# Output, attention output, up and down projections by seven half-size products, with the mixing on GpSimd

## The chip, the cores and the metric

One core of a Trainium2 chip runs the kernel in one launch. The metric is the device time of that launch in microseconds. TensorE (PE) does the matmuls into PSUM, its weight loads (PEld) run beside them; VectorE (DVE), ScalarE (ACT) and GpSimd (POOL) work elementwise; SyncE (SP) issues most DMAs.

## The reference

A decoder block for 512 tokens and a width of 1024, all in float32:

```python
h = rmsnorm(x, norm_mix_g);  proj = h @ w_in           # 1024 -> 5120 + 3 * 1024
branches = stack([conv_out, sb_out, ret_out])           # three mixers of width 512
merged = sum(sigmoid(gates) * (branches @ w_branch))
x = x + merged @ w_o                                    # 1024 x 1024
h = rmsnorm(x, norm_xa_g)
x = x + memory_attention(h, mem_n, w_xq, w_xkv, w_out)  # w_out: 1024 x 1024
h = rmsnorm(x, norm_mlp_g)
x = x + square(relu(h @ w_up)) @ w_down                 # 1024 -> 4096 -> 1024
return rmsnorm(x, final_g)
```

## The kernel before, in words

**Precision.** Every large product is made of three matmuls in a fast float32 format: each operand is split into a high part (a cast on ScalarE) and a low part (a subtraction on VectorE), and high x high, high x low and low x high are added in PSUM. `split` (L221) does this for activations, `parts_of` (L103) for weights: ScalarE writes the high part at L111, VectorE subtracts at L112. `mm3` (L232) issues the three matmuls.

**Weights.** They come as blocks of 128x1024 (512 KB) from SyncE's queue into `w_raw` (three buffers). `Stream` lists all blocks in the order of their use; `run_plan` (L203) goes through the plan of work items, and ahead of each item prepares the weights up to two steps beyond what the item needs (`AHEAD`). A block of kind `Plain` is one step, one `parts_of`. A block of kind `Seven` is two loads and four steps; two of them mix weights first: `combo` (L134) forms two differences of 512 columns on VectorE into `w_mix`.

**Two ways to multiply.** `proj_t` (weights stationary, 128x512 or 128x256 matmuls) and `proj_m` (tokens stationary, 512 weight columns moving) take all products as they are. `seven` (L282) makes two blocks of 128 output columns from seven half-size products instead of eight (rows of the weight, columns and tokens are halved; sums and differences of the halves are multiplied, and the results added). It takes its mixed activations from `Mixes`, made once per normed input on VectorE, and uses 128x256 matmuls (L290). Half of the gate columns and 24 of the 32 up columns go that way.

**The stages that the change touches**, in order:
- gates: `gated` (L722) sums the three gated branches into `mg` and splits the sum into `mgs`.
- output projection: `proj_norm` (L842) runs `items_m` (L322) over `w_o` twice, once for each half of the 1024 output columns: four row blocks of tokens, eight blocks of 128 weight rows, three matmuls of 128x512 each. All eight accumulate in PSUM, and then VectorE adds the bank into `x` (L836): eight adds for each 1024 rows of weight and 512 columns. Then the norm and the transposes follow for each block of tokens.
- cross attention: `xa_out` (L937) makes the heads' outputs and splits them; `proj_norm` runs again, over `w_xo`.
- MLP: the up columns come in rounds of eight (`first_up`, `up7`), each followed by `items_m` over 1024 rows of `w_down`. The up results go through relu, a square and a split into `u`.
- end: the last pass over `w_down` goes by token blocks, so that `final` (L1028) norms and stores one block while TensorE does the next.

The order of instructions on each engine is settled when the program is built, by a scheduler that starts from the order of the plan. An engine goes through its list in order.

## Time and profile before

| | us |
|---|---|
| median of three runs (1033.85 to 1033.92) | 1033.91 |
| the profiled execution, its own time | 1033.71 |
| its span, first to last instruction | 1032.0 |
| output projection, from its first to its last matmul | 472 to 520 |
| cross-attention output projection | 637 to 682 |
| matmuls of the down projection | 729 to 1025 |

A row of a table of windows gives a stretch of the span, its length, and then for each engine the busy time in it with the number of instructions. A row of a timeline gives start, duration, engine, line, operation, what is written and read, and in brackets the idle time before it and what ended it. Names are those of tiles in the program: `w_raw` and `w_mix` are weights before the split, `w_part` after it, `mm` and `p` are PSUM banks, `sb_`, `r_` and `cv_` belong to the three mixers. "128x512" is partitions by elements.

### The profile page before, as it was taken

The numbers are of one execution on the slowest core, as the hardware profiler recorded it, in microseconds if no ns is written. First come the engines' busy times: TensorE is split into PE (matmuls) and PEld (weight loads), VectorE is DVE, ScalarE is ACT, GpSimd is POOL, SyncE is SP. The second block draws the span as 40 slices with busy tenths as digits, with TensorE's granted clock in tenths as the row PEclk, the third lists the DMA queues.
The fourth block names the chain that finished last, engine by engine and source line by source line (L and its number), as shares of the span: only waits on it lengthen the run. The fifth ranks groups of instructions, "written<-read, shape, count | busy, mean of one in ns | idle before, by whom it ended". The sixth has DMA issues, their size and how long they took to land.

```text
span 1032.0 us, 14325 instructions
## 1 busy us (share of the span) xinstructions
PE 1015.5 (98%) x5636; PEld 884.9 (86%) x5636; DVE 648.8 (63%) x992; ACT 500.7 (49%) x887; POOL 66.2 (6%) x118
## 2 busy tenths in 40 slices
PE   6999999999999999999999999999999999999997
PEld 4888888888888889998898888898889989989985
DVE  5567777856563796784584555466947566565643
ACT  6465567766532154463463444345416624643741
POOL 1101112321110000000100000000000000000000
PEclk9999999999999999999999999999999999999999
DMA  6322233213122212335354213223222321332222
GB/s 265 103 102 81 83 104 102 82 42 123 62 87 79 100 62 83 103 119 198 133 184 163 82 47 118 81 83 123 86 79 82 125 92 71 124 123 80 103 85 81
DMA packets 29876, 106.33 MB, mean 103 GB/s; under 512 B 3569, under 2 KB 3569, under 8 KB 29809
## 3 DMA queue, kind: packets, MB, share of 16 engines
q1 hardware_dynamic: 27216, 98.05, 27.7%
q10 hardware_dynamic: 2592, 7.37, 2.0%
q8 instruction: 44, 0.72, 0.3%
q14 instruction: 24, 0.19, 0.1%
HBM read 103.31 MB, written 2.10 MB: 102 GB/s over the span
## 4 chain that ended last, share of the span: by engine, by line
PE 97%; DMA 1%; DVE 0%; ACT 0%; SPq 0%; issue 0%; DVEq 0%; POOLq 0%; POOL 0%
PE mm L235 24%; PE mm L234 24%; PE mm L236 24%; PE p L290 17%; PE at L385 1%; PE o L546 1%; PE aT L512 1%; DMA w_raw<-in_w_in_dram 1%; PE z L488 1%; PE z L489 0%; PE xsc L236 0%; PE xsc L235 0%; PE xsc L234 0%; PE ro L693 0%; PE sc L667 0%; PE xpp L929 0%
## 5 line engine op out<-in xcount | busy, mean ns | idle before, releaser
L112 DVE TENSOR_TENSOR w_part<-w_raw,w_part 128x1024 fp32r<-128x1024 f32 (+1 forms) x180 | 210.9, 1176 | 168.1 <-PE mm L235 75.2
L111 ACT CAST w_part<-w_raw 128x1024 fp32r<-128x1024 f32 (+1 forms) x180 | 180.6, 1006 | 135.2 <-PE mm L236 79.1
L234 PE MATMUL mm<-hT_h,w_part 128*128 128x512 f32 (+1 forms) x512 | 193.6, 379 | 0.0
L235 PE MATMUL mm<-hT_l,w_part 128*128 128x512 f32 (+1 forms) x512 | 193.3, 378 | 0.0
L236 PE MATMUL mm<-hT_h,w_part 128*128 128x512 f32 (+1 forms) x512 | 193.0, 378 | 0.0
L290 PE MATMUL p<-mix_h,w_part 128*128 128x256 f32 x576 | 112.2, 283 | 0.5 <-ACT sv_s L297 0.5
L236 PEld LDWEIGHTS mm<-hT_h,w_part 128*128 128x128 f32 x512 | 96.4, 188 | 17.1
L234 PEld LDWEIGHTS mm<-hT_h,w_part 128*128 128x128 f32 x512 | 96.2, 188 | 16.8
L235 PEld LDWEIGHTS mm<-hT_l,w_part 128*128 128x128 f32 x512 | 96.5, 188 | 16.4
L235 PE MATMUL mm<-w_part,u_h 128*128 128x512 f32 x256 | 99.8, 390 | 0.0
L234 PE MATMUL mm<-w_part,u_h 128*128 128x512 f32 x256 | 98.6, 390 | 0.0
L236 PE MATMUL mm<-w_part,u_l 128*128 128x512 f32 x256 | 98.2, 389 | 0.0
L290 PEld LDWEIGHTS p<-mix_h,w_part 128*128 128x128 f32 x576 | 93.4, 192 | 1.4 <-ACT sv_s L297 0.7
L290 PE MATMUL p<-hT_h,w_part 128*128 128x256 f32 x432 | 84.4, 283 | 0.0
L290 PE MATMUL p<-mix_l,w_part 128*128 128x256 f32 x288 | 81.5, 283 | 0.0
L290 PEld LDWEIGHTS p<-hT_h,w_part 128*128 128x128 f32 x432 | 70.1, 192 | 0.8
L111 ACT CAST w_part<-w_mix 128x1024 fp32r<-128x1024 f32 x36 | 37.8, 1051 | 55.9 <-PE mm L235 37.5
L112 DVE TENSOR_TENSOR w_part<-w_mix,w_part 128x1024 fp32r<-128x1024 f32 x36 | 44.0, 1221 | 26.7 <-ACT w_part L111 20.0
L290 PE MATMUL p<-hT_l,w_part 128*128 128x256 f32 x216 | 60.7, 283 | 0.0
L236 PEld LDWEIGHTS mm<-w_part,u_l 128*128 128x128 f32 x256 | 48.1, 188 | 9.8
L235 PEld LDWEIGHTS mm<-w_part,u_h 128*128 128x128 f32 x256 | 48.1, 188 | 9.5
L234 PEld LDWEIGHTS mm<-w_part,u_h 128*128 128x128 f32 x256 | 47.9, 188 | 9.5
(211 smaller groups left out, 1813.2 us busy)
## 6 DMA issues: line engine op xcount, KB each, us to landing
w_raw<-in_w_in_dram SPq DMA_DIRECT2D x52, 512.0 KB, 3.4
w_raw<-in_w_up_dram SPq DMA_DIRECT2D x32, 512.0 KB, 3.6
w_raw<-in_w_down_dram SPq DMA_DIRECT2D x32, 512.0 KB, 3.4
w_raw<-in_w_br_dram SPq DMA_DIRECT2D x12, 512.0 KB, 3.4
w_raw<-in_w_gate_dram SPq DMA_DIRECT2D x12, 512.0 KB, 3.5
w_raw<-in_w_o_dram SPq DMA_DIRECT2D x8, 512.0 KB, 3.5
w_raw<-in_w_xk_dram SPq DMA_DIRECT2D x8, 512.0 KB, 4.2
w_raw<-in_w_xv_dram SPq DMA_DIRECT2D x8, 512.0 KB, 3.5
```

The lines of the kernel that those rows point to most:

```text
L111: act.copy(out=wh, in_=src)
L112: dve.tensor_tensor(out=wl, in0=src, in1=wh.bitcast(F32), op=ALU.subtract)
L234: te.matmul(ps, lh, rh, start=first, stop=False)
L235: te.matmul(ps, lh, rl, start=False, stop=False)
L236: te.matmul(ps, ll, rh, start=False, stop=last)
L290: te.matmul(ps[:, :256], x[:, k, :], y, start=first and k == 0 and i == 0, stop=k == 3 and i == 2, skip_group_check=True)
L385: te.transpose(ps[:, k * P:(k + 1) * P], xn[:, c * P:(c + 1) * P], ident)
L488: te.matmul(z[:, :s], q[:, e, tsl], S["skh", hp][:, e, :s], start=True, stop=False)
L512: te.transpose(aps[:, sb * P:(sb + 1) * P], a[:, sb * P:(sb + 1) * P], ident)
L546: te.matmul(dst, vv, rhs, start=sb == 0 and i == 0, stop=sb == nblk and i == 1, skip_group_check=True)
```

## The change

The weights `w_o`, `w_xo` and `w_down` are now taken in rounds of 512 rows, and each round by seven half-size products (rows of the weight by 256, output columns by 512, tokens by 256). Tokens are stationary and 512 weight columns move, so the matmuls stay 128x512: 7 x 12 of them a round in place of 96.
- `Wide` prepares a round's weights: four loads, seven steps, each with a `parts_of` of 1024 columns; four additions or subtractions of 128x1024 mix them first, on GpSimd, partly in place in `w_raw`.
- `Pairs` holds the activations of a round for the products; `make` mixes two blocks of 128 rows with one GpSimd instruction of 512 elements and two of 256, and splits the results (three times 512, once 256).
- `items_w` issues the products P1 to P7, each for two blocks of 128 tokens. P1, P6, P7 and P4 accumulate one after another in one PSUM bank for each token block, P5 and P3 in another, P2 has its own. After each product VectorE adds the bank, as it stands, into one quarter of `x`: 14 adds of 128x512 a round.
- `Seven` has its four weight combinations on GpSimd, too; its first product's signs are turned so that ScalarE has one copy less.
- The up columns go in pairs, and a round of `w_down` follows every second pair; the square of relu is taken on ScalarE. The four plain up columns that ran with 512 tokens at once run in two halves of 256, since hT now lies in blocks of 256 tokens (`Blocks`).
- The end norms two token blocks together. `w_raw` has four buffers for three, `w_part` ten for eleven. The weights are packed to suit.

```diff
@@ -31,7 +31,7 @@
...
-RAWS, WBUFS, AHEAD = 3, 11, 2
+RAWS, WBUFS, AHEAD = 4, 10, 2
...
+    def minus(out, a, b):
+        pool.tensor_tensor(out=out, in0=a, in1=b, op=ALU.subtract)
+    def plus(out, a, b):
+        pool.tensor_tensor(out=out, in0=a, in1=b, op=ALU.add)
+    def mix_raw():
+        return wpool.tile([P, CW], F32, name="w_mix", bufs=2)
...
-        def combo(self, a0, a1, b0, b1):
-            x = wpool.tile([P, CW], F32, name="w_mix", bufs=2)
-            dve.tensor_tensor(out=x[:, :512], in0=a0, in1=a1, op=ALU.subtract)
-            dve.tensor_tensor(out=x[:, 512:], in0=b0, in1=x[:, :512] if b1 is None else b1, op=ALU.subtract)
-            return x
...
         def s1(self, raw):
-            ra, rb = raw
-            self.x1 = self.combo(ra[:, 512:], ra[:, :512], rb[:, :512], ra[:, 512:])
-            return parts_of(self.x1)
+            l, r = raw[0][:, :512], raw[0][:, 512:]
+            b22, b21 = raw[1][:, :512], raw[1][:, 512:]
+            self.x = mix_raw()
+            minus(l, r, l)
+            plus(r, r, b22)
+            plus(self.x[:, :512], b22, l)
+            minus(self.x[:, 512:], b21, self.x[:, :512])
+            return parts_of(raw[0])
         def s2(self, raw):
-            rb = raw[1]
-            return parts_of(self.combo(rb[:, :512], self.x1[:, :512], rb[:, 512:], None))
+            return parts_of(self.x)
...
+    ORDER = ("P1", "P5", "P6", "P3", "P2", "P7", "P4")
...
+    class Wide:
...
+        def __init__(self, t, c):
+            self.loads = [(t, c + i) for i in range(4)]
+            self.need = (1, 2, 3, 3, 4, 4, 4)
+            self.steps = [lambda raw, n=n: self.step(raw, n) for n in range(7)]
+            self.parts = []
+        def step(self, raw, n):
+            src = raw[(0, 0, 0, 2, 3, 1, 0)[n]]
+            if n == 1:
+                minus(raw[0], raw[1], raw[0])
+            elif n == 2:
+                src = self.x = mix_raw()
+                plus(src, raw[2], raw[0])
+                plus(raw[1], raw[1], raw[2])
+            elif n == 6:
+                src = self.x
+                minus(src, raw[3], src)
+            return parts_of(src)
...
-                    self.steps.append((e, st, first + (len(e.loads) if i else 1)))
+                    self.steps.append((e, st, first + e.need[i]))
...
+    class Pairs:
+        def __init__(self):
+            self.b = unit("pr_b", (P, 2, 2, 256))
+            self.w = [{}, {}]
+        def make(self, e, s, u):
+            def put(names, src):
+                w = unit("pr", (P, 2, 2, 256))
+                split(w[:, 0], w[:, 1], src)
+                for i, n in enumerate(names):
+                    self.w[e][n] = w[:, 0, i, :], w[:, 1, i, :]
+            v = scr("pr_v", (P, 2, 256))
+            pool.tensor_tensor(out=v, in0=u[:, 0:1, :].broadcast_to([P, 2, 256]), in1=s, op=ALU.subtract)
+            put(("A11", "A22"), s)
+            minus(u[:, 0, :], s[:, 0, :], v[:, 1, :])
+            put(("S3", "S1"), v)
+            hi, lo = self.w[e]["A12"] = self.b[:, e, 0, :], self.b[:, e, 1, :]
+            split(hi, lo, u[:, 1, :])
+            minus(u[:, 1, :], u[:, 1, :], u[:, 0, :])
+            put(("S2", "S4"), u)
...
+    LEFT = dict(P1="A11", P2="A12", P3="S4", P4="A22", P5="S1", P6="S2", P7="S3")
+    TO = dict(P1=(0, 0), P2=(0, 0), P3=(0, 1), P4=(2, 0), P5=(2, 1), P6=(0, 1), P7=(2, 1))
...
+    def items_w(src, c, pairs, after=lambda p: None):
...
+        acc = {}
+        for n, p in enumerate(ORDER):
+            def fn(w, p=p):
+                wh, wl = wv(w, 2)
+                blocks = pairs().w
+                for i in range(2):
+                    if p == "P2":
+                        ps = mmps("p2")
+                    else:
+                        bank = "p3" if p in ("P5", "P3") else "p1"
+                        if p in ("P1", "P5"):
+                            acc[bank, i] = atps(bank)
+                        ps = acc[bank, i]
+                    tok = slice(i * P, (i + 1) * P)
+                    for k in range(2):
+                        ah, al = [x[:, tok] for x in blocks[k][LEFT[p]]]
+                        for m, (x, y) in enumerate(((ah, wh), (ah, wl), (al, wh))):
+                            te.matmul(ps, x, y[:, k, :], start=p in ("P1", "P5", "P2") and k == 0 and m == 0,
+                                      stop=k == 1 and m == 2, skip_group_check=True)
+                    t, h = TO[p]
+                    dst = S["x"][t + i][:, h * 512:(h + 1) * 512]
+                    dve.tensor_tensor(out=dst, in0=ps, in1=dst, op=ALU.add)
+            item(fn, (Wide, src, c, n + 1))
+            after(p)
...
-        if n == 2:
-            if d % 2 == 0:
-                S["mgs", d // 2] = [unit("mgs") for _ in range(2)]
-            hi, lo = S["mgs", d // 2]
-            split(hi[:, d % 2, :], lo[:, d % 2, :], m)
+        if n == 2 and d % 2 == 1:
+            q = d // 2
+            if q % 2 == 0:
+                S["mp", q // 2] = Pairs()
+            m = S.pop(("mg", q)).rearrange("p e (h t) -> p (e h) t", h=2)
+            S["mp", q // 2].make(q % 2, m[:, 0:4:3, :], m[:, 1:3, :])
...
-    def proj_norm(src, a, g, after):
-        items_m(src, 0, a, add_x(0))
...
+    def proj_norm(src, pairs, g, between, after, parts=lambda: Split("hT", KT)):
...
+        items_w(src, 0, lambda: pairs(0))
+        between()
...
+        def ends(p):
+            if p == "P3":
...
+                    for t in (0, 1):
+                        norm_begin(t, S["x"][t], 1)
+                item(begin)
+            if p == "P2":
+                item(lambda: [norm_end(t, S["x"][t], S["g"], 0) for t in (0, 1)])
+            if p == "P7":
+                item(lambda: [norm_begin(t, S["x"][t], 1) for t in (2, 3)])
+                item(lambda: norm_T(0, S["hT"], 0))
+            if p == "P4":
+                item(lambda: [norm_end(t, S["x"][t], S["g"], 0) for t in (2, 3)])
+                item(lambda: norm_T(1, S["hT"], 1))
+        items_w(src, 4, lambda: pairs(1), ends)
+        after(lambda t: item(lambda: norm_T(t, S["hT"], t)))
...
-    proj_norm(w_o, lambda: mgs, g_xa, kv_proj)
+    proj_norm(w_o, lambda i: S["mp", i], g_xa, lambda: None, kv_proj)
...
     def xa_out(h):
-        if h == 0:
-            S["xo"] = Split("xo", KT)
+        if h % 2 == 0:
+            S["xo", h // 2] = Pairs()
...
-            hi, lo = S["xo"](d)
-            split(hi, lo, ps)
+            act.copy(out=(u if e else s)[:, e, :], in_=ps[:, LH])
+            act.copy(out=(s if e else u)[:, e, :], in_=ps[:, RH_])
+        S["xo", h // 2].make(h % 2, s, u)
...
+    def u_ready(q, s, u):
+        act.activation(out=s, in_=s, func=AF.Square)
+        act.activation(out=u, in_=u, func=AF.Square)
+        if q % 2 == 0:
+            S["u", q // 2] = Pairs()
+        S["u", q // 2].make(q % 2, *[x.rearrange("p (a b) -> p a b", a=2) for x in (s, u)])
...
+    def up_half(w, d, half_, pss):
+        if half_ == 0:
+            pss[d] = mmps()
+        proj_t(pss[d][:, 256 * half_:256 * half_ + 256], w, S["hT"].half(half_))
+        if half_ == 1:
+            up_done(d)(pss[d])
...
+    def up_plain(q):
+        for d in (2 * q, 2 * q + 1):
+            pss = {}
+            item(lambda w, d=d, pss=pss: [up_half(w, d, i, pss) for i in range(2)], (Plain, w_up, d))
+    def up7(q):
+        def fn(w):
+            s, u, p1 = seven(w, S["mix"])
+            act.activation(out=u[:, LH], in_=p1[:, LH], func=AF.Relu)
+            act.activation(out=s, in_=s, func=AF.Relu)
+            act.activation(out=u[:, RH_], in_=u[:, RH_], func=AF.Relu)
+            u_ready(q, s, u)
+        item(fn, (Seven, w_up7, 2 * q - U7))
+    proj_norm(w_xo, lambda i: S["xo", i], g_mlp, lambda: item(lambda: xa_out(3)), first_up, lambda: Blocks("hT"))
...
-    item(final_begin)
-    its = capture(lambda: items_m(w_down, 28, lambda: S["u"], add_x(1), tok_outer=True))
-    for t in range(NT):
...
+    def last(p):
...
+        if p == "P2":
+            item(lambda: [final(t) for t in (0, 1)])
...
+        if p == "P4":
+            item(lambda: [final(t) for t in (2, 3)])
...
+    def down(r):
+        items_w(w_down, 4 * r, lambda: S["u", r], last if r == NP // 2 - 1 else lambda p: None)
+    for q in range(2, NP):
+        if q < U7 // 2:
+            up_plain(q)
+        else:
+            up7(q)
+        if q == 2:
+            mix_items()
+        if q % 2 == 0 and q < NP - 2:
+            down(q // 2 - 1)
+    down(NP // 2 - 2)
+    down(NP // 2 - 1)
...
+    b = w.reshape(-1, 2, 2, P, 2, 512)
+    blocks = [b[:, :, k, :, c] for k, c in ((0, 0), (0, 1), (1, 1), (1, 0))]
+    return np.stack(blocks, axis=1).transpose(0, 1, 3, 2, 4).reshape(-1, P, CW)
```

The order of the built program shows what this moves. GpSimd, from the retention stage to the end of the program, before (`r_qd` and `rstd` are of retention and of the norms):

```order
L675 TENSOR_TENSOR r_qd<-r_qk,dqd 128x512 x2
L348 TENSOR_TENSOR rstd<-r_ve,half 128x4 x2
L675 TENSOR_TENSOR r_qd<-r_qk,dqd 128x512 x2
L348 TENSOR_TENSOR rstd<-r_ve,half 128x4 x2
L348 TENSOR_TENSOR rstd<-ms,half 128x1 x14
```

Behind retention it had only 14 reciprocal roots of one column. Now, in the middle of the MLP (the weights of one pair of up columns, then of one round of `w_down`, with the up results `sv_s` and `sv_u` between):

```order
L143 TENSOR_TENSOR w_raw<-w_raw 128x512
L146 TENSOR_TENSOR w_raw<-w_raw 128x512
L146 TENSOR_TENSOR w_mix<-w_raw 128x512
L143 TENSOR_TENSOR w_mix<-w_raw,w_mix 128x512
L143 TENSOR_TENSOR w_raw<-w_raw 128x1024
L385 TENSOR_TENSOR pr_v<-sv_u,sv_s 128x512
L146 TENSOR_TENSOR w_mix<-w_raw 128x1024
L146 TENSOR_TENSOR w_raw<-w_raw 128x1024
L143 TENSOR_TENSOR sv_u<-sv_s,pr_v 128x256
L143 TENSOR_TENSOR w_mix<-w_raw,w_mix 128x1024
L143 TENSOR_TENSOR sv_u<-sv_u 128x256
```

All of these read only SBUF. VectorE in the middle of the MLP, before (`w_mix` rows are the combinations, `w_part` rows the low parts of weights, `sv` and `x` rows add from PSUM):

```order
L137 TENSOR_TENSOR w_mix<-w_raw 128x512
L836 TENSOR_TENSOR x<-mm,x 128x512 x3
L112 TENSOR_TENSOR w_part<-w_mix,w_part 128x1024
L136 TENSOR_TENSOR w_mix<-w_raw,w_mix 128x512
L137 TENSOR_TENSOR w_mix<-w_raw,w_mix 128x512
L303 TENSOR_TENSOR sv_7751<-p_7747,sv_s 128x256
L308 TENSOR_TENSOR sv_7752<-p_7748,sv_u 128x256
L112 TENSOR_TENSOR w_part<-w_raw,w_part 128x1024
L112 TENSOR_TENSOR w_part<-w_raw,w_part 128x512
L306 TENSOR_TENSOR sv_7752<-sv_s,sv_u 128x256
```

And at such a place now (`pr` rows are the low parts of mixed activations, `x<-p` rows the adds after each product):

```order
L360 TENSOR_TENSOR sv_s<-p_7960,sv_s 128x256
L422 TENSOR_TENSOR x<-p_8082,x 128x512
L422 TENSOR_TENSOR x<-p_8090,x 128x512
L128 TENSOR_TENSOR w_part<-w_raw,w_part 128x1024
L280 TENSOR_TENSOR pr<-pr_v,pr 128x512
L364 TENSOR_TENSOR sv_u<-p_7961,sv_u 128x256
L362 TENSOR_TENSOR sv_s<-p_7959,sv_s 128x256
L128 TENSOR_TENSOR w_part<-w_mix,w_part 128x1024
L422 TENSOR_TENSOR x<-p_8102,x 128x512
L128 TENSOR_TENSOR w_part<-w_raw,w_part 128x1024 x3
L280 TENSOR_TENSOR pr<-sv_u,pr 128x512
L422 TENSOR_TENSOR x<-p_8110,x 128x512
```

The combinations are gone from VectorE's list; adds and splits stand between one another. TensorE, from P7 to P4 at the end of a round (buffer numbers kept: `p1_9638` and `p1_9646` are the banks of the two token blocks, `pr` are stationary):

```order
L418 MATMUL p1_9638<-w_part_9692,pr_9477 128x512
L418 MATMUL p1_9646<-w_part_9692,pr_9341 128x512
L418 MATMUL p1_9646<-w_part_9693,pr_9341 128x512
L418 MATMUL p1_9646<-w_part_9692,pr_9341 128x512
L418 MATMUL p1_9646<-w_part_9692,pr_9477 128x512
L418 MATMUL p1_9646<-w_part_9693,pr_9477 128x512
L418 MATMUL p1_9646<-w_part_9692,pr_9477 128x512
L418 MATMUL p1_9638<-w_part_9721,pr_9337 128x512
```

The last row is the first matmul of P4: it writes the bank that P7 filled six matmuls earlier, so it comes behind VectorE's add of that bank.

More of the change, by code (lines that the diff above doesn't have):

```diff
@@ L79, in span, with __init__, half @@
             return self.h[u][:, o:o + n, sl], self.l[u][:, o:o + n, sl]
+    class Blocks:
+        per = 4
+        def __init__(self, name):
+            self.h = [[unit(name + "_h", (P, 4, 256)) for _ in range(2)] for _ in range(2)]
+            self.l = [[unit(name + "_l", (P, 4, 256)) for _ in range(2)] for _ in range(2)]
+        def span(self, k, n, sl):
+            t, o = sl.start // 256, sl.start % 256
+            sl = slice(o, o + sl.stop - sl.start)
+            return tuple(x[k // 4][t][:, k % 4:k % 4 + n, sl] for x in (self.h, self.l))
+        def half(self, t):
+            return lambda k: (self.h[k // 4][t][:, k % 4, :], self.l[k // 4][t][:, k % 4, :])
     ident = const.tile([P, P], F32, name="ident")
@@ L205, in run_plan @@
         for chunks, _ in plan:
[L206 removed]
+            for kind, t, c, *_ in chunks:
                 k = (t.tensor.name, c)
@@ L279, in __getitem__ @@
             k0, t0 = dict(A11=(0, 0), A12=(4, 0), A22=(4, 256))[n]
-            return [[p[:, t0:t0 + 256] for p in self.a(k0 + k)] for k in range(4)]
+            return [[p[:, 0, :] for p in self.a.span(k0 + k, 1, slice(t0, t0 + 256))] for k in range(4)]
     def seven(b, a):
```

158 lines of the change are left out of this document (61 added, 97 removed).

## The prediction

> **What bounds the kernel now.** I read the page's busy shares first, then the chain of work that ended last.
>
> ```profile
> PE 1015.5 (98%) x5636; PEld 884.9 (86%) x5636; DVE 648.8 (63%) x992; ACT 500.7 (49%) x887; POOL 66.2 (6%) x118
> PE 97%; DMA 1%; DVE 0%; ACT 0%; SPq 0%; issue 0%; DVEq 0%; POOLq 0%; POOL 0%
> ```
>
> TensorE carries the whole chain. Matmuls overlap, so their price is the distance between starts, not their duration. I read it from TensorE's timeline in the last down projection (44 starts from first to last row) and from the chain in a run of half-width products.
>
> ```profile
> 1014.85 0.39 PE L234 MATMUL mm<-w_part,u_h 128*128 128x512 f32 x1
> ...
> 1024.59 0.39 PE L235 MATMUL mm<-w_part,u_h 128*128 128x512 f32 x1
> 942.72 30.47 PE p L290 x254
> ```
>
> A 128x512 costs 9.74 / 43 = 0.2265 us, a 128x256 costs 30.47 / 254 = 0.120 us. A matmul removed is worth that much, for as long as the other engines keep up. Whether they do is read by stage. The table of windows covers the attention output projection, the cross-attention output projection, and the MLP from its second half-pass to the last add.
>
> ```profile
> core 0: us, PE busy (x) PEld busy (x) DVE busy (x) ACT busy (x) POOL busy (x), PEclk, DMA share, GB/s
> 478.70:533.00 54.30, 54.30 (x306) 47.43 (x305) 36.91 (x61) 26.52 (x56) 3.32 (x6) 1.00 0.52 185
> 630.00:676.00 46.00, 46.00 (x212) 38.25 (x211) 20.08 (x31) 14.90 (x29) 1.10 (x2) 1.00 0.24 81
> 700.00:1026.00 326.00, 324.72 (x1934) 290.10 (x1932) 200.50 (x275) 150.62 (x252) 1.65 (x3) 1.00 0.28 97
> ```
>
> In the MLP VectorE works 200.5 of 326 us and GpSimd 1.65. That is the cover that the change spends.
>
> **TensorE's side of the change.** A round of 512 rows takes 7 x 12 = 84 matmuls of 128x512 in place of 96. There are 2 + 2 + 8 = 12 rounds: 144 x 0.2265 = 32.6 us go. Four up columns now run in two halves: 192 x 0.120 in place of 96 x 0.2265, which adds 1.3 us. TensorE alone would give 1033.7 - 31.3 = 1002.4 us. Of this, 21.7 - 1.3 = 20.4 us lie in the MLP's window, which TensorE could then pass in 305.6 us.
>
> **VectorE's side.** Its price, too, is the distance between starts where it isn't idle. Its timeline shows:
>
> ```profile
> 187.21 0.69 DVE L502 TENSOR_TENSOR sb_suf<-z,sb_suf 128x512 f32<-128x512 f32 x1
> 187.81 0.68 DVE L613 TENSOR_TENSOR r_qk<-mm,rot 128x512 f32<-128x512 f32 x1
> 188.41 1.22 DVE L112 TENSOR_TENSOR w_part<-w_raw,w_part 128x1024 fp32r<-128x1024 f32 x1
> ...
> 198.19 0.42 DVE L502 TENSOR_TENSOR sb_suf<-z,sb_suf 128x256 f32<-128x256 f32 x1
> 198.53 0.68 DVE L613 TENSOR_TENSOR r_qk<-mm,rot 128x512 f32<-128x512 f32 x1
> ...
> 212.88 1.23 DVE L112 TENSOR_TENSOR w_part<-w_raw,w_part 128x1024 fp32r<-128x1024 f32 x1 [0.35 <-PE mm L235]
> 214.02 1.22 DVE L500 TENSOR_TENSOR_SCAN sb_suf<-ones,sb_e 128x512 f32<-128x512 f32 x1
> ```
>
> 512 columns cost 0.60 us, 256 cost 0.34, 1024 cost 1.14. In the MLP: 112 adds into x for 32 (14 a round for 4), +48.0; 24 more weight splits of 1024 (7 a round for 4), +27.4; 48 weight combinations leave for GpSimd, -28.8; splitting the mixed activations costs 16 x (3 x 0.60 + 0.34) = 34.2 where 32 splits and 8 squares cost 24.0, +10.2. VectorE's own work rises by 56.8 to 257.3 us. Against 305.6 that alone would still fit.
>
> **GpSimd's side, and what it takes from VectorE.** The MLP puts on GpSimd 32 additions of 1024 columns (four a round), 64 of 512 and 32 of 256. The trace has two-input work on GpSimd only at 512 columns, and beside it VectorE's timeline is telling:
>
> ```profile
> 160.33 1.23 DVE L500 TENSOR_TENSOR_SCAN sb_suf<-ones,sb_e 128x512 f32<-128x512 f32 x1 [0.46 <-POOL sb_e L479]
> 160.49 2.16 POOL L612 TENSOR_TENSOR r_sw<-r_sw,rot 128x512 f32<-128x512 f32 x1 [0.19 <-POOL sb_e L479]
> 162.20 1.52 DVE L112 TENSOR_TENSOR w_part<-w_raw,w_part 128x1024 fp32r<-128x1024 f32 x1
> ...
> 186.59 1.67 POOL L612 TENSOR_TENSOR r_sw<-r_sw,rot 128x512 f32<-128x512 f32 x1 [0.68 <-ACT r_sw L611]
> ...
> 265.21 1.30 POOL L675 TENSOR_TENSOR r_qd<-r_qk,dqd 128x512 f32<-128x512 f32 x1
> 265.75 1.84 DVE L112 TENSOR_TENSOR w_part<-w_raw,w_part 128x1024 fp32r<-128x1024 f32 x1
> ```
>
> The split at 265.75 takes 1.84 in place of 1.22 and ends 1.08 us after GpSimd's end at 266.51. The split at 162.20 ends 1.07 after GpSimd's end at 162.65. GpSimd in turn, started under the scan that ends at 161.56, stretches from 1.30 to 2.16 and ends 1.09 after it. They don't share, they take turns: a VectorE instruction with both inputs in SBUF and a GpSimd instruction exclude one another, for 1.07 us (VectorE, 1024) and 1.09 us (GpSimd, 512). The two quoted above at 187.21 and 187.81 ran beneath GpSimd's 186.59 at their usual 0.69 and 0.68: each has one input in PSUM. So adds into x and adds of products are free of it; splits of weights and mixed activations aren't.
>
> GpSimd's unseen sizes: a 1024 can't hold the turn less than a 512 (1.09), nor longer than two full 512 instructions (2.60); I take 2.18, in proportion, as VectorE's durations nearly double from 0.69 to 1.23. A 256 lies between the 128-column select below (0.29) and 1.09; I take 0.55.
>
> ```profile
> 199.21 0.29 POOL L479 TENSOR_SCALAR_AFFINE_SELECT sb_suf<-sb_suf 128x128 f32<-128x128 f32 x1
> ```
>
> [...]
>
> GpSimd's turns in the MLP: 32 x 2.18 + 64 x 1.09 + 32 x 0.55 = 157 us. VectorE's excluding turns at 1.07 per 1024: 100 full weight splits 107.0, 12 half ones 6.4, mixed activations 48 x 0.535 + 16 x 0.27 = 30.0, the 24 instructions that mix hT 12.8; together 156 us. The sum, 313 us, is already over TensorE's 305.6. And 313 needs every one of VectorE's other 257 - 156 = 101 us to fall beneath a GpSimd turn. VectorE goes through its list in order, so it runs free only until its next split; the rows of the change show splits and adds mixed about one to one. I take 0.7 of the 101 as hidden: VectorE is blocked 157 - 71 = 86 us, and the MLP takes 257 + 86 = 343.6 us where it took 326: **+17.6**. Ends: all hidden 313 (-13), four tenths hidden 374 (+48); with GpSimd's 1024 at 1.09 the turns shrink by 35 and TensorE bounds at 305.6 (-20), at 2.60 they grow by 13 (+31).
>
> [...]
>
> **The two attention projections.** Each gets 6 more splits (6.8) and 12 more adds (7.2) on VectorE, GpSimd turns of 8 x 2.18 = 17.4 and 24 matmuls less (-5.4). First stage: VectorE 36.9 + 14.0 = 50.9 plus some 2.4 blocked (most of its other work hides the turns) against TensorE's 48.9: 53.3 for 54.3, **-1**. Second: 20.1 + 14.0 + 2.1 of mixed activations = 36.2, plus 5.6 blocked (19.6 of turns, 0.7 x 20 hidden) = 41.8 against TensorE's 40.6; with a wait or two for a bank 43 for 46, **-3**. Ends: -5.4 each, or +5 each.
>
> **The rest.** The gate stage moves its 24 combinations to GpSimd; TensorE has no gap there and VectorE gains slack: nothing, and at worst the 24 turns of 1.09 if they came to TensorE's door. Loads are as many and as large (DMA share 0.28 above); the fourth raw buffer lets them wait on the in-place mixing at no cost as long as VectorE isn't late. ScalarE's 150.6 us in the MLP grow by 24 casts and stay far under 300. At the end two row blocks finish together rather than one: **+1** for a second norm.
>
> Sum against the profiled run's 1033.71 us (span 1032.0; the median of the three is 1033.91): 1033.7 + 17.6 - 1 - 3 + 1 = **1048 us**.
>
> **Rivals.** *The turns fall into place* (faster, 0.27). If 0.9 to all of VectorE's other work lies beneath GpSimd's turns, or GpSimd's wide additions are cheaper than in proportion, the MLP takes 306 to 322 and the attention stages give 5 each: 1002 to 1030. The mechanism decides at 0.83 hidden, where 257 + 157 - 84 = 330 only just offsets the attention stages' gain. For it: adds stand between splits all through the list, and GpSimd is needed only half the time. Against it: 313 of turns in 306 us leave no room at all. *Bank hand-offs* (slower still, 0.25). The last product of a round writes the bank of the one before it, and so does the next round's first; TensorE may start only when VectorE has added the earlier one. The cover is the six matmuls of the other row block, 6 x 0.2265 = 1.36 us. An add behind one blocked split is 2.18 + 1.14 + 0.60 = 3.9 us late, 2.6 over the cover; an undisturbed one is in time. Two hand-offs a round, 12 rounds, half of 2.6 each: +31 on the forecast, 1079. For it: VectorE will have little idle time. Against: the order puts up products between hand-offs in six rounds.
>
> **How the numbers follow.** Forecast 0.42 (1036 to 1062), bank hand-offs 0.25 (1062 to 1095), the turns falling into place 0.27 (1002 to 1030), in between and within 0.2% 0.06; 0.2% is about what a measurement of this kernel can tell from no change. Faster 0.27, same 0.06, slower 0.67. The likeliest case by itself spans 1036 to 1062. For 8 in 10 the range must take in most of both rivals: 1010 to 1085, which also holds both ends of GpSimd's price.
>
> **What would show it.** Right: in the MLP TensorE has gaps that VectorE's splits end; splits of 1024 average 1.5 us or more in place of 1.23; GpSimd's additions of 512 lie above 1.30; adds into x stay at 0.69. Wrong: TensorE busy to 98% again with a span near 1005; or splits still at 1.23 beside a busy GpSimd, which would mean that the turns are no exclusion; or gaps ended by raw loads.

## The result, and the profile after

The changed kernel takes 1140.09 us (median of four, 1138.98 to 1140.99) where the kernel before takes 1033.88 beside it: a ratio of 1.1027, 95% interval 1.1008 to 1.1046. The profiled execution's span is 1138.7. The prediction was 1048 us with a range of 1010 to 1085; slower was right, the size was not.

First the page of the changed kernel: busy time by engine, TensorE's granted clock in 40 slices, and the shares of the chain that ended last.

```profile
PE 1024.8 (90%) x5588; PEld 881.5 (77%) x5588; DVE 849.8 (75%) x1108; ACT 561.4 (49%) x983; POOL 403.6 (35%) x310
PEclk9999999999999999958999998998999899899989
PE 61%; DVE 18%; issue 9%; POOL 5%; ACT 4%; DMA 2%; SPq 0%; ACTq 0%; DVEq 0%; POOLq 0%
```

TensorE falls from 98% to 90% of a longer span. It does 144 matmuls of 128x512 less, worth 32.6 us, and yet is busy 9 us longer: the clock row is no longer all nines. The chain, 97% TensorE before, now goes through every engine.

To see where, I cut both spans at the same four events: the first gate product in seven parts, the first cross-attention score, the last transpose of scores, and the last transpose of the MLP's norm.

| stretch | before | after | |
|---|---|---|---|
| start to first gate product in seven parts | 380.3 | 381.6 | +1.3 |
| gates' second half, output projection, keys and values | 192.5 | 229.7 | +37.2 |
| queries, cross attention | 58.7 | 65.4 | +6.7 |
| its output projection, first up products | 61.0 | 65.2 | +4.2 |
| MLP from the last norm transpose to the end | 339.5 | 396.8 | +57.3 |

So two places make 94.5 of the 106.7 us: the MLP and the stretch with the output projection. These are the last stretch's rows in the table of windows, before and then after.

```profile
692.50:1032.00 339.50, 332.22 (x1996) 297.60 (x1994) 205.06 (x283) 153.88 (x258) 2.20 (x4) 1.00 0.28 95
```

```profile
741.90:1138.70 396.80, 338.15 (x1994) 297.22 (x1992) 334.83 (x361) 192.92 (x317) 227.84 (x132) 0.94 0.24 80
```

After the length come the busy times of PE, PEld, DVE, ACT and POOL, then the granted clock. VectorE is busy 334.8 us, but of 396.8: it idles 62 us, and TensorE idles 58.6. Over the stretch as a whole no engine is full. The groups of VectorE and GpSimd in that stretch:

```profile
L128 DVE TENSOR_TENSOR w_part<-w_raw,w_part 128x1024 fp32r<-128x1024 f32 x67 | 113.9, 1706 | 15.0 <-ACT w_part L127 15.0
L146 POOL TENSOR_TENSOR w_raw<-w_raw 128x1024 f32<-128x1024 f32 x8 | 25.4, 3173 | 0.0
L143 POOL TENSOR_TENSOR w_raw<-w_raw 128x1024 f32<-128x1024 f32 x8 | 21.2, 2650 | 36.7 <-DVE w_part L128 36.7
```

A split of a raw weight block takes 1.71 us on average (one of a mixed block 1.31) where it took 1.22. A GpSimd addition of 1024 columns takes 2.65 to 3.17 in the means of its four groups, where an undisturbed one took 2.40. The timeline shows both being held up, VectorE in the first block of rows, GpSimd in the second:

```profile
915.71 1.27 DVE L422 TENSOR_TENSOR x<-p,x 128x512 f32<-128x512 f32 x2
916.90 3.15 DVE L128 TENSOR_TENSOR w_part<-w_raw,w_part 128x1024 fp32r<-128x1024 f32 x1
919.98 2.82 DVE L280 TENSOR_TENSOR pr<-pr_v,pr 128x512 fp32r<-128x512 f32 x1
```

```profile
753.27 2.40 POOL L143 TENSOR_TENSOR w_raw<-w_raw 128x1024 f32<-128x1024 f32 x1 [21.72 <-DVE w_part L128]
...
916.57 2.41 POOL L146 TENSOR_TENSOR w_mix<-w_raw 128x1024 f32<-128x1024 f32 x1
918.93 3.32 POOL L146 TENSOR_TENSOR w_raw<-w_raw 128x1024 f32<-128x1024 f32 x1
```

The split at 916.90 waits out GpSimd's addition until 918.98 and ends 1.07 after it; the next addition is held for the split, takes 3.32 and ends 2.20 after it (at 922.25); the activation split behind it waits for that in turn, takes 2.82 in place of 0.69 and ends 0.55 after the addition. The two adds into `x` at 915.71, with one input in PSUM, are not touched.

### The profile page after: what moved, and what is told of

Same layout as the page of the kernel before. It is cut to its first block, busy times and chain, and to the rows that moved or that the text cites. A ratio compares the mean times of both kernels' runs of the same rounds, so it can differ in the third digit from the quotient of the medians.

```text
span 1138.7 us, 14827 instructions
## 1 busy us (share of the span) xinstructions
PE 1024.8 (90%) x5588; PEld 881.5 (77%) x5588; DVE 849.8 (75%) x1108; ACT 561.4 (49%) x983; POOL 403.6 (35%) x310
## 4 chain that ended last, share of the span: by engine, by line
PE 61%; DVE 18%; issue 9%; POOL 5%; ACT 4%; DMA 2%; SPq 0%; ACTq 0%; DVEq 0%; POOLq 0%
PE mm L291 13%; PE mm L292 13%; PE mm L290 13%; PE p L418 8%; PE p L348 7%; DVE w_part L128 6%; DVE x L422 4%; DVE pr L280 3%; ACT w_part L127 2%; POOL w_mix L143 1%; DVE pr_b L280 1%; POOL w_raw L143 1%; PE o L660 1%; DMA m_sb<-in_mem_dram 1%; POOL w_raw L146 1%
## 5 line engine op out<-in xcount | busy, mean ns | idle before, releaser
L128 DVE TENSOR_TENSOR w_part<-w_raw,w_part 128x1024 fp32r<-128x1024 f32 (+1 forms) x210 | 289.9, 1385 | 109.3 <-ACT w_part L127 93.2
L127 ACT CAST w_part<-w_raw 128x1024 fp32r<-128x1024 f32 (+1 forms) x210 | 211.5, 1011 | 210.5 <-PE mm L291 101.5
L418 PE MATMUL p<-w_part,pr 128*128 128x512 f32 x864 | 232.0, 419 | 45.3 <-DVE sv_u L364 18.2
L418 PEld LDWEIGHTS p<-w_part,pr 128*128 128x128 f32 x864 | 171.0, 204 | 88.7 <-DVE x L422 14.1
L290 PE MATMUL mm<-hT_h,w_part 128*128 128x512 f32 (+1 forms) x544 | 199.0, 368 | 2.1 <-ACT w_part L127 1.9
L292 PE MATMUL mm<-hT_h,w_part 128*128 128x512 f32 (+1 forms) x544 | 198.9, 366 | 0.0
L143 POOL TENSOR_TENSOR w_raw<-w_raw 128x512 f32<-128x512 f32 (+1 forms) x30 | 56.3, 1878 | 183.4 <-DVE w_part L128 183.4
L422 DVE TENSOR_TENSOR x<-p,x 128x512 f32<-128x512 f32 x168 | 109.8, 679 | 12.3 <-PE p L418 12.2
L290 PEld LDWEIGHTS mm<-hT_h,w_part 128*128 128x128 f32 x544 | 102.3, 189 | 17.8 <-ACT w_part L127 2.3
L292 PEld LDWEIGHTS mm<-hT_h,w_part 128*128 128x128 f32 x544 | 102.6, 189 | 16.1
L143 POOL TENSOR_TENSOR w_mix<-w_raw,w_mix 128x512 f32<-128x512 f32 (+1 forms) x30 | 64.8, 2160 | 22.6 <-DVE w_part L128 16.5
L128 DVE TENSOR_TENSOR w_part<-w_mix,w_part 128x1024 fp32r<-128x1024 f32 x42 | 57.1, 1360 | 20.1 <-ACT w_part L127 15.4
L146 POOL TENSOR_TENSOR w_raw<-w_raw 128x512 f32<-128x512 f32 (+1 forms) x30 | 64.0, 2134 | 1.3
```

Source lines behind the costliest of these rows:

```text
L127: act.copy(out=wh, in_=src)
L128: dve.tensor_tensor(out=wl, in0=src, in1=wh.bitcast(F32), op=ALU.subtract)
L143: pool.tensor_tensor(out=out, in0=a, in1=b, op=ALU.subtract)
L146: pool.tensor_tensor(out=out, in0=a, in1=b, op=ALU.add)
L290: te.matmul(ps, lh, rh, start=first, stop=False)
L292: te.matmul(ps, ll, rh, start=False, stop=last)
```

## The experiments

All are edits of the changed kernel unless said otherwise, timed against the kernel before on the same chip (1033.7 to 1033.8 us). "MLP" is the last stretch of the table above.

### The MLP: what GpSimd's mixing costs, taken apart

**No mixing** (`e1_no_mix`). `minus` and `plus` do nothing, the steps split what was loaded, and the activations go unmixed into their splits; the output is not the reference's.

```diff
 def minus(out, a, b):
-    pool.tensor_tensor(out=out, in0=a, in1=b, op=ALU.subtract)
+    pass
+plus = minus
...
-                src = self.x = mix_raw()
+                src = raw[2]
```

> GpSimd's mixing is left out: the weight splits take a raw block as loaded and the activation splits take the unmixed activations, so products use wrong blocks and the output is not the reference's; every load, split, product and add stays. Theory A (the mixing on GpSimd, by its turns with VectorE, is what makes the MLP late): from the last norm's transposes to the end 305 to 315 us where the changed kernel takes 396.8, VectorE's 1024-column weight splits at 1.23 us, and the whole at 1045 to 1062 us, since the stall ahead of the memory norm (about 30 us) stays. Theory D (the product rounds' own hand-offs, an add of VectorE after each six products, make it late): the MLP stays above 340 and the whole above 1085.

1041.56 us, MLP 321.5:

```profile
718.20:1039.70 321.50, 312.40 (x1994) 284.10 (x1992) 256.93 (x361) 195.18 (x317) 2.58 (x4) 0.99 0.30 99
```

TensorE alone would need 339.5 - 20.4 = 319.1 there, so the rounds, with 112 adds in all and seven splits each, cost only 2.4 us by themselves; the 305 to 315 that I had written were too low, and the total lies just below its range. Mixing on GpSimd costs the MLP 396.8 - 321.5 = 75.3 us.

**GpSimd as long, but not reading** (`e2_memset`).

```diff
+    c = (slice(None),) * (len(out.shape) - 1) + (slice(0, 1),)
-    pool.tensor_tensor(out=out, in0=a, in1=b, op=ALU.subtract)
+    pool.tensor_tensor(out=out[c], in0=a[c], in1=b[c], op=ALU.subtract)
+    for _ in range(2):
+        pool.memset(out, 0.01)
+plus = minus
```

> Each GpSimd addition is replaced by one of a single column (which keeps the waits for its inputs) and two fills of its whole output with a constant, so that GpSimd is about as long busy at the same places but hardly reads; the mixed blocks hold a constant and the output is not the reference's. Turns as the cause: VectorE's splits fall back to 1.23 us and the total is within 20 us of the run without mixing (1045 to 1080). GpSimd's latency in the chain from its inputs to the casts as the cause: GpSimd's operation lasts as long, so the total stays above 1115 with splits at 1.23.

1072.08 us, MLP 343.0. First its window row, then the splits of raw weight blocks in the MLP:

```profile
726.80:1069.80 343.00, 321.38 (x1994) 286.46 (x1992) 259.48 (x361) 190.97 (x317) 194.07 (x388) 0.99 0.28 93
```

```profile
L128 DVE TENSOR_TENSOR w_part<-w_raw,w_part 128x1024 fp32r<-128x1024 f32 x67 | 81.9, 1224 | 22.4 <-ACT w_part L127 22.1
```

GpSimd is busy 194 us of the stretch, about the 183 that its additions take undisturbed (32 x 2.40 + 64 x 1.30 + 32 x 0.73), and VectorE's splits stay at 1.22 us, where they took 1.71 beside the changed kernel's additions: GpSimd's additions take turns with VectorE, its fills, which only write, don't. So GpSimd's time in the chain that leads to a product (load, split, addition, cast, split) costs 343.0 - 321.5 = 21.5 us without any turn; the total lies in the range given for turns as the cause, but 30.5 us above the run without mixing and not within 20.

**Turns without the chain** (`e8_turns`, `e9_turns_const`). As without mixing, but GpSimd makes its additions into a buffer that nobody reads:

```diff
 def minus(out, a, b):
-    pool.tensor_tensor(out=out, in0=a, in1=b, op=ALU.subtract)
...
+    x = mix_raw()[:, :b.shape[-1] * (b.shape[1] if len(b.shape) == 3 else 1)]
...
+    pool.tensor_tensor(out=x, in0=a, in1=b, op=ALU.subtract)
```

In the second run the additions for the weights read a constant `c`, the block of ones; those for the activations are as in the first:

```diff
+    if len(b.shape) == 3 or b.shape[-1] == 256:
+        pool.tensor_tensor(out=x, in0=a, in1=b, op=ALU.subtract)
+    else:
+        pool.tensor_tensor(out=x, in0=c, in1=c, op=ALU.subtract)
```

> The run without mixing, but GpSimd makes all its additions from the same inputs at the same places of its list and writes them to a buffer that nobody reads: turns with VectorE, and no chain through GpSimd. The output is not the reference's, as in the run without mixing. By the prediction's sum VectorE is blocked for 86 us beyond its own 257: MLP 335 to 345, against 321.5 without the turns and 396.8 with turns and chain, total 1055 to 1068. Turns alone as the whole cost: MLP above 385, total above 1105. Turns as nothing by themselves: MLP under 328.

> As the run with turns and without chain (its additions are read by nobody, its output is not the reference's), but the additions that stand for the weight blocks' mixing read a constant block, so that they neither wait for a raw block nor hold its buffer; those on the activations still read these, and set the pace of GpSimd's list. If the run before was late by raw buffers held behind GpSimd's list (ScalarE waited 77 us there for loads that had no buffer), the MLP falls from 391.9 to 335 to 350, what the prediction's sum gives for turns alone. If the turns do it by themselves, the MLP stays above 380.

The first took 1126.93 us, MLP 391.9, which looks like turns alone. But two rows of its waits between 760 and 1100 us (in total, times, longest) show another cause:

```profile
POOL w_mix L146 <- ACT sv_u L1100: 67.2, 10, 10.5
ACT w_part L127 <- DMA w_raw<-in_w_up_dram: 63.5, 7, 12.3
```

GpSimd's list waits for activations, the raw blocks whose additions stand behind such a wait hold their buffers, and ScalarE waits for loads that have none. With the constant in their place 1093.05 us with an MLP of 354.6 are left, a little above the 335 to 350 expected. Its window row, then what ended most of TensorE's idle time between 760 and 1090 us:

```profile
737.00:1091.60 354.60, 320.77 (x1994) 286.83 (x1992) 327.00 (x361) 195.34 (x317) 231.69 (x132) 0.98 0.28 90
```

```profile
PE p L426 <- DVE x L430: 21.3, 12, 6.2
```

VectorE is busy 327.0 - 256.9 = 70 us longer than without mixing, and the MLP is 33.1 us longer. TensorE waits there for VectorE's late adds into `x`. So by these two stand-ins turns cost 33.1 us and the chain 21.5; the changed kernel has 75.3, and 20.7 come only where both meet.

TensorE's clock accounts for a good part of that rest. From half-microsecond slices of the MLP, TensorE's busy time multiplied by what its granted clock lacks to 1 comes to 0.0 us without mixing, 1.7 with the chain alone, 4.4 with turns alone and 19.5 in the changed kernel: 13.5 us come only where both meet. This is an account of the traces; no run here holds the clock fixed.

**Everything on VectorE** (`e4_dve`).

```diff
-    pool.tensor_tensor(out=out, in0=a, in1=b, op=ALU.subtract)
+    dve.tensor_tensor(out=out, in0=a, in1=b, op=ALU.subtract)
```

> The same mixing, every addition of it on VectorE in place of GpSimd. Turns as the cause: VectorE's own work in the MLP becomes 257 + 32 x 1.14 + 64 x 0.60 + 32 x 0.34 = 343 us with nothing to take turns with, so the MLP takes 343 to 360 where it takes 397, and the total is 1085 to 1105: faster than with GpSimd. Latency through in-order lists as the cause: a longer VectorE list delays adds and splits more; the total is 1140 or above.

1096.13 us, MLP 360.0 with VectorE busy 339.4: 44 us faster than with GpSimd's help.

**Half of it on VectorE** (`e11_pairs_dve`: activations; `e12_weights_dve`: weights). The same edit, in `Pairs.make` alone, and everywhere else alone.

> The changed kernel with the activations' mixing (three additions for each pair of columns) on VectorE, the weights' mixing still on GpSimd. GpSimd then never waits for an activation, 139 of its 183 us of additions in the MLP stay, and VectorE gets 16 x (0.60 + 2 x 0.34) = 20 us more work. If a good part of the loss is GpSimd's list, where weight mixing stands behind an activation that is not there yet and holds its raw blocks: the MLP falls from 396.8 to 360 to 380, the total to 1103 to 1123. If the turns' sheer time is what counts: less of it by 44 but 20 more on VectorE, the MLP within 12 us of 396.8, the total above 1128.

> The other half: the weights' mixing on VectorE, the activations' on GpSimd. VectorE's own work in the MLP is 257 + 32 x 1.14 + 48 x 0.60 = 322 us; GpSimd's 44 us block it for at most 44. If GpSimd's list with two kinds of work in it is the cause, nothing waits behind an activation here but another activation: MLP at or under the 360.0 of the run with all mixing on VectorE (345 to 362), total 1080 to 1098. If each GpSimd addition costs by its turns and its hop alike: MLP 365 to 380, total 1100 to 1118.

The first took 1142.55 us, MLP 394.1; the second 1097.94, MLP 359.0:

```profile
746.60:1140.70 394.10, 338.11 (x1994) 296.29 (x1991) 355.63 (x409) 194.09 (x317) 160.51 (x84) 0.94 0.25 81
```

```profile
737.20:1096.20 359.00, 322.60 (x1994) 285.20 (x1992) 338.94 (x441) 195.67 (x317) 69.72 (x52) 0.98 0.27 89
```

With all on GpSimd the MLP took 396.8, with all on VectorE 360.0. So the 36.8 us that GpSimd costs more than VectorE lie with the weights' mixing; the activations' mixing costs about the same on either engine. The two runs tell which work costs, not by what. In the first, GpSimd waits for no activation, and the MLP is only 2.7 us shorter; but VectorE is busy 355.6 us there, 20.8 more than in the changed kernel, and may have lost what GpSimd's list gained. The second lies where a list with two kinds of work as the cause was expected to put it (345 to 362).

**More lead, another order** (`e6_ahead3`, `e7_order`, the second with the blocks' order and a norm's transposes moved to suit).

```diff
-RAWS, WBUFS, AHEAD = 4, 10, 2
+RAWS, WBUFS, AHEAD = 4, 10, 3
```

```diff
-ORDER = ("P1", "P5", "P6", "P3", "P2", "P7", "P4")
+ORDER = ("P1", "P5", "P6", "P3", "P7", "P2", "P4")
```

> The changed kernel with its weight steps issued three ahead of the products rather than two. Latency through the chain of raw block, GpSimd, cast, split and product as what turns stretch: one step more of lead takes 15 us or more off the MLP's 396.8 and the total is 1100 to 1125. VectorE's list as the bound: the same work in the same lists, the MLP within 5 us of 396.8 and the total 1133 to 1145; the same if the ten buffers of split blocks are what bounds the lead.

> P2, which writes a bank of its own, stands between P7 and P4, which write the same bank, where it stood ahead of P7 (and the first norm transpose moves behind P4 in the two attention projections). Bank hand-offs as a main cost: twelve products more of cover at P4's hand-off save up to 2.6 us in each of 8 rounds, MLP 375 to 387 and total 1118 to 1130. If hand-offs are no main cost: MLP within 5 us of 396.8, total 1135 to 1145.

1139.96 and 1142.40 us, MLP 396.6 and 396.5. The first says nothing of the lead. In its trace every engine goes through the changed kernel's instructions in the changed kernel's order (5588 matmuls, 1108 instructions on VectorE, 310 on GpSimd), and the engines are busy the same in the MLP to within 0.2 us:

```profile
742.40:1139.00 396.60, 337.95 (x1994) 297.07 (x1992) 334.85 (x361) 192.98 (x317) 227.90 (x132) 0.94 0.24 80
```

The order is settled when the program is built, and it came out the same. Whether more lead would help stays untested. The second does move instructions: P4's hand-off has twelve matmuls more of cover, the next round's first product has not, and the MLP doesn't change.

### Fewer rounds

From the kernel before: only the four middle rounds of the down projection in seven products, mixing on VectorE (`f1_half_dve`) or on GpSimd (`f2_half_pool`).

```diff
-    for r in range(4):
-        up7(r)
-        items_m(w_down, 8 * r, lambda: S["u"], add_x(0))
+    WIDE = (1, 2)
...
+        for k in late:
+            items_w(w_down, 4 * k, lambda k=k: S["pu", k])
```

> The kernel before, with the seven products only in the down projection's four middle rounds of 512 rows, and all their mixing on VectorE. TensorE does 48 products of 128x512 less: 48 x 0.2265 = 10.9 us, 1023 if nothing else moves. VectorE's work in the MLP: 205 + 16 x 1.14 for mixing, 12 x 1.14 for more weight splits, 40 x 0.60 for more adds, 8 x 3.42 - 16 x 0.60 for activations = 279 us of 329. If a mix costs little as long as VectorE has slack and no turns are taken: 1023 to 1030, faster than before. If the rounds' chains and the lower clock after gaps take the gain all the same: 1034 to 1045.

> The same four rounds, with their 40 additions on GpSimd: 16 x 2.40 + 8 x (1.30 + 2 x 0.73) = 60 us there, and 29 us less on VectorE. By count of engine time this is the better place, and without turns it would be 1020 to 1028. With turns: a third of the GpSimd time of the changed kernel's MLP, so about a third of its 75 us over the run without mixing, 25 us: 1040 to 1052, and slower than the run with VectorE by 10 or more.

1041.37 us (ratio 1.0074, 1.0060 to 1.0087) and 1061.19 (1.0272, 1.0258 to 1.0286). TensorE alone would need 1033.7 - 10.9 = 1022.8. The run with VectorE is 18.6 us above that; the run with GpSimd is 38.4 above it, where a third of 75 had promised 25. Sixty us of GpSimd's additions are dearer by 20 than 29 us of the same on VectorE. With VectorE, the sum itself came out: it is busy 274.0 us of the MLP's 347.8, where I had 279 of 329. But the mean over the MLP was the wrong measure. The table of windows of that run:

```profile
692.50:770.00 77.50, 77.50 (x407) 66.91 (x406) 51.95 (x73) 30.33 (x44) 0.00 (x0) 1.00 0.28 89
...
810.00:850.00 40.00, 37.90 (x244) 34.07 (x243) 39.03 (x57) 22.58 (x39) 0.00 (x0) 1.00 0.30 95
850.00:890.00 40.00, 36.79 (x227) 32.55 (x226) 39.32 (x56) 23.82 (x41) 0.00 (x0) 1.00 0.31 103
```

In the rounds with seven products (810 to 970) VectorE is busy 37 to 40 of each 40 us; the 25 us that it has to spare before 770 don't help there. The slack that counts is that of the round.

### The output projection: where TensorE stood still

TensorE's timeline of the changed kernel there, then ScalarE's:

```profile
485.62 4.24 PE L418 MATMUL p<-w_part,pr_b 128*128 128x512 f32 x10 [0.65 <-DVE w_part L128]
507.14 1.94 PE L499 MATMUL at<-ident,xn 128*128 128x128 f32 x8 [17.28 <-DVE xn L490]
516.23 1.94 PE L499 MATMUL at<-ident,xn 128*128 128x128 f32 x8 [7.16 <-DVE xn L490]
```

```profile
491.15 0.62 ACT L279 CAST pr<-mg 128x512 fp32r<-128x512 f32 x1
491.16 1.79 ACTq L115 DMA_DIRECT2D x<-in_x_dram  x4
492.99 0.47 ACTq L109 DMA_DIRECT2D g_bc<-in_g_mem_dram  x1
493.49 0.47 ACTq L932 DMA_DIRECT2D m_sb<-in_mem_dram  x1
503.51 0.63 ACT L468 ACTIVATE xn<-m_sb 128x512 f32<-128x512 f32 x1 [11.74 <-DMA m_sb<-in_mem_dram]
```

After the first product TensorE's list has the transposes of the memory norm. Their load was issued at 493.49 only, behind the casts of the mixed activations and the four loads of `x`. And behind the norm in the lists stand the products, which need `x` from 491.16 for their first add.

**The norm later; also `x` earlier** (`e3_mem`, `e5_x_early`, the second on top of the first).

```diff
-    item(mem_norm)
-    proj_norm(w_o, lambda i: S["mp", i], g_xa, lambda: None, kv_proj)
+    proj_norm(w_o, lambda i: S["mp", i], g_xa, lambda: item(mem_norm), kv_proj)
```

```diff
-    item(reload_x)
...
+                if (n, q, e) == (2, KT // 2 - 1, 0):
+                    reload_x()
                 d = 2 * q + e
```

> Only the memory norm moves: from ahead of the output projection's first round to between its two rounds. Theory B (TensorE stands still there because the norm's transposes, next in its list, wait for a late load): the stretch from the last gate product to the first cross-attention score falls from 128.7 to 98 to 106 us and the total by 23 to 31, to 1109 to 1117. Rival (the round itself is that late, by its reload of x and its mixing): the stretch falls by less than 10 us, total above 1130.

> On top of the moved memory norm, the four loads of x are issued before the activation blocks of the last gate column are cast, where in that run they stood behind these casts on ScalarE's queue and arrived at 506.8 us. If TensorE's 17.2 us wait there for VectorE's first add into x is the load, it falls to 4 to 8 us and the total from 1132.2 by 9 to 13, to 1119 to 1124. If the mixing on GpSimd holds the round up anyway, the total stays within 3 us of 1132.

The norm's move gave 7.9 us only (1132.17), not the 23 to 31 of the theory that it alone was the cause: `x` came later still, and TensorE waited for the first add.

```profile
503.11 0.62 ACT L279 CAST pr<-mg 128x512 fp32r<-128x512 f32 x1 [8.53 <-POOL mg L143]
503.12 1.78 ACTq L115 DMA_DIRECT2D x<-in_x_dram  x4
```

```profile
507.54 12.58 PE L418 MATMUL p<-w_part,pr 128*128 128x512 f32 x42 [17.24 <-DVE x L422]
```

The four loads stand behind a cast that waits for GpSimd's mixing. Issued at 484.47, ahead of it, they took another 7.4 us off: 1124.75, just above the range. TensorE's longest wait for an add into `x` there is 2.5 us. Both together bring the stretch from 229.7 to 214.2.

**Both, and no mixing** (`e10_no_mix_early`: the three edits together).

> No mixing on GpSimd, as in the first run (the output is not the reference's), and in the output projection the memory norm between the rounds and x loaded early. If the stall there and the mixing are all that keeps the changed kernel from what TensorE alone would need (1002 us by the prediction), the stretch from the first gate product in seven parts to the first cross-attention score falls from 216.0 to 192 to 200 us and the total from 1041.6 to 1017 to 1026, the rest being 2 us of hand-offs in the MLP and the first rounds' wait for x. If the stretch stays above 208, the round structure itself (14 adds into x, x needed after the first twelve products) holds the stage up, and the total is above 1033.

1030.02 us (1027.26 to 1030.57; ratio 0.9965, 0.9950 to 0.9979), the stretch 203.0, between the two cases. With nothing mixed at all, and so with a wrong output, the rounds are worth 0.35%. Of the stretch's 37.2 us, leaving out the mixing takes away 13.7 (216.0 in the first run above) and moving norm and loads then 13.0; 10.5 stay lost against the kernel before. One wait of TensorE for the memory norm, from 502.1 on, still takes 7.2 us in this trace; the DMA engines moved 0 GB/s from 502.0 to 503.0 and 139 to 418 from there to 509.0. No version here that computes the reference beats the kernel before.

## Why the prediction was wrong

- **TensorE's side** held. With no mixing the MLP takes 321.5 us for the 319.1 that follow from the sum.
- **VectorE's own work** held: 257.3 in the prediction's window, 4.6 more in this stretch (205.1 - 200.5), and 256.9 measured without mixing.
- **Turns** held as a mechanism, and their price nearly: 78 us blocked (334.8 - 256.9) for the 86 worked out, 70 in the run with turns alone. GpSimd's turn of 1024, which the prediction had no row for and put at 2.18, is 2.20 in the timeline above. With turns alone the MLP took 354.6; the forecast of +17.6 makes 357.1 of this stretch's 339.5. That is nearer than the sum deserves, since VectorE was busy 327.0 us there and not all the time. Of the four signs named, splits of 1024 came to 1.59 on average (113.9 + 36.8 us for 95 of them), GpSimd's 512 to 1.35 and more, adds into `x` stayed at 0.68; but TensorE's gaps were ended by adds of products, adds into `x` and casts of mixed activations more than by splits. What TensorE waited for longest in the MLP (in total, times, longest):

```profile
PE p L418 <- DVE sv_u L364: 18.2, 6, 4.8
PE p L418 <- DVE x L422: 9.7, 5, 3.4
PE p L418 <- ACT pr L279: 9.1, 3, 4.0
```

- **The step that failed** is "VectorE is blocked 157 - 71 = 86 us, and the MLP takes 257 + 86 = 343.6". It takes VectorE's busy time for the stage's time. VectorE was busy 334.8 us, and the stage took 396.8. A mixed weight goes from its load through a split (which the mixing in place waits for), GpSimd, a cast and another split to its product; GpSimd's time in that chain costs 21.5 us when nobody blocks anybody, turns without it 33.1, both together 75.3. The prediction had no term for the chain and none for their meeting. Of the last 20.7 us, 13.5 go with TensorE's lower clock by the account above; the rest is open. That stretched additions and splits add up along the chain is argued only.
- **TensorE's clock** was not in the sum: 19.5 us in the MLP. Of the 75.3 us, 49.5 are more idle time (58.6 - 9.1) and 25.8 more busy time, most of it this.
- **The output projection**, "53.3 for 54.3, -1", went to +37.2 with the gates beside it. It was costed by the engines' busy time alone. That TensorE now needs the first add into `x` early (in the run with the norm moved it comes to a stop after 36 of the products' matmuls, where the kernel before made its first add after 78), and that the casts of mixed activations stand ahead of the loads of `x` and of the memory, was overlooked: "at no cost" was said of the weight blocks' loads and not asked of ScalarE's queue. Moving the two gave back 15.3 us.
- **The cross-attention stages.** The second projection was put at -3; its stretch measured +4.2, and the stretch ahead of it, for which there was no term, +6.7. Without mixing the two take 60.7 and 60.1 for 58.7 and 61.0 before: 9.8 of the 10.9 us are again the mixing.
- **Bank hand-offs**, the rival at 1079, are not the main cost: adds into `x` ended 9.7 of TensorE's 58.6 idle us, where the rival's price makes 21 for the MLP's eight rounds, and more cover at one of a round's two hand-offs changed nothing (396.5 for 396.8). But they are how turns reach TensorE when the chain is out of the way (21.3 us in the run with turns alone). The rival of turns that fall into place means 56 to 66 us blocked (157 - 101 to 157 - 91); 78 lie between it and the forecast, and 396.8 refutes its 306 to 322.

## What to carry to other kernels

Work moved to an idle engine is priced by three things: what it blocks while it runs, what its time adds to the chain that leads to the bound engine, and what both do together, that engine's lower clock after gaps among it; here 33, 21 and 21 us in the MLP, of which the prediction had the first alone. Slack is counted per round and not over a stage's mean. When a result is needed earlier than before (an add into `x` after a few products in place of a whole pass), ask at once where its inputs' loads stand in their queue. And when an edit changes nothing, compare the order of instructions before reading the time: the edit may not have reached the program.

## What the runs showed of the hardware

**With gaps of 4.03 and 3.31 us TensorE's granted clock fell to 0.50, and it stayed there for some 5 and 3 us after.** The changed kernel, TensorE's timeline and then its windows (busy time and count, granted clock):

```profile
890.31 5.36 PE L418 MATMUL p<-w_part,pr 128*128 128x512 f32 x12 [4.03 <-ACT pr L279]
923.19 2.93 PE L418 MATMUL p<-w_part,pr 128*128 128x512 f32 x6 [3.31 <-DVE sv_u L364]
```

```profile
888.00:892.00 4.00, 1.69 (x4) 0.57 0.10 40
892.00:896.00 4.00, 4.00 (x14) 0.57 0.02 4
896.00:900.00 4.00, 4.00 (x30) 1.00 0.38 131
```

Twelve matmuls after a gap of 4.03 us took 5.36 where 12 x 0.2265 and a last end 0.16 later give 2.88; six after a gap of 3.31 took 2.93 for 1.52. After one gap of 1.70 us next to nothing was lost, as the run with early loads shows (18 x 0.2265 + 0.16 = 4.24):

```profile
501.94 4.37 PE L418 MATMUL p<-w_part,pr 128*128 128x512 f32 x18 [1.70 <-DVE x L422]
```

The length of a gap doesn't decide it alone here. After a gap of 2.32 us (until 873.17) the clock stayed at 1.00, while one of 1.89 (until 1103.30) was followed by some 3.4 us at half, which began when TensorE was running again:

```profile
1102.40:1102.90 0.50, 0.00 (x0) 1.00 1.07 328
1102.90:1103.40 0.50, 0.10 (x1) 1.00 0.86 295
1103.90:1104.40 0.50, 0.50 (x2) 0.50 0.23 90
```

So two waits were paid for a second time: 2.5 and 1.4 us after the gaps of 4.03 and 3.31 us.

**GpSimd's fills did not hold up VectorE's splits, its additions did**: fills of 128x1024 took 0.95 us beside splits at 1.22, while additions stretched splits of raw blocks to 1.71 and were themselves stretched from 2.40 to as much as 3.17 in the mean of a group.
